# Eight changes at once in the front of a transformer block: chunks of 128 instead of 127 tokens, reordered loads, gate products in column tiles, a longer look-ahead for weight buffers

## Chip, cores, metric

One Trainium2 chip, one program on all 8 of its cores. Times are device microseconds (us) of the slowest core. Cores 0 to 3 are one die, 4 to 7 the other. In some executions, whatever the kernel, one die runs at a lower granted clock and the program takes some per cent longer (the slow state); such runs are set apart, and fast runs are compared with fast runs.

## The reference

A decoder block on `x` of 4 x 2048 x 2048, float32:

```
h = RMSNorm(x)
[B, C, u | q, k, v, o, i, f] = h @ W_in             # i, f: 4 gate columns each
y_m = sigmoid(o) * headnorm(mLSTM(q, k, v, i, f))   # 4 heads, state carried along the sequence
x  += concat(B * conv3(C * u), y_m) @ W_out
x  += W_down(silu(g) * u),  [g, u] = conv3(RMSNorm(x) @ W_up) + b
x  += sigmoid(RMSNorm(x) @ W_pg) * (p @ W_pp)       # the last stage ("PLE")
out = RMSNorm(x)
```

The mLSTM is a linear recurrence with exponential gates: the state that a later token sees is a gated sum of `v_s k_s^T` over all earlier tokens.

## The kernel before

Core `2b + half` has batch `b` and one half of its sequence (1032 tokens with an overlap of 8). Nothing is exchanged between cores. A core of the second half must know the state at the end of the first half, so every core first works through the 1016 tokens before its own (the prefix; zeros for the first half). The front, 0 to some 180 us, runs in this order:

1. Prefix: 8 chunks of 127 tokens. Per chunk: 16 one-column products that sum the squares (for the RMSNorm), 16 products of 8 columns for the gates, 2 x 16 products of 256 columns for the keys (weights k0 and k1), 16 transposes of x.
2. The core's own tokens, half 0: squares on ScalarE, summed on TensorE; logarithm and exponential for 1/rms; sixteen VectorE operations that scale x to h; gate products; then the key unit k0.
3. The big product G = x^T k (16 x 8 products of 512 columns), at position 21 to 28 of the weights' schedule.
4. Rest of the key units, gate mathematics, C = G^T W_v for head 0 (weights v0), then the unit o0. From there to the end the work is mostly bound by TensorE.

The prefix, cut:

```python
LP, NPCH = 127, PT // LP                     # PT = 1016: 8 chunks
def prefix_k(pump):
    slab_load(1, [k1.loads[1]])              # slab c: x of chunk c; slab 1 waits for two loads of k1
    slab_load(2, [k1.loads[3]])              # slab 2 for all of k1
    for c in range(3, 7): slab_load(c)
    ...
    for c in range(NPCH):
        for k in range(16): mm(PS[0:P_, 6, c:c+1], sqd[:, k, :], ones_bf[:, 0:1], ...)           # 127 weights, 1 column
        if c == 0:
            ... own_load(0, f) ... own_load(1, f)       # own x, 2 x 16 transfers
            own.squares(0); Norm.blocks(own, H1, 0, ... own.gates ...)   # queued for ScalarE, VectorE, TensorE
        for k in range(16): mm(PS[0:P_, 6, 16+8*c:24+8*c], hTp[:, c, k, 0:P_], wif[:, k, :], ...) # 8 columns
        for half in range(2):
            for k in range(8*half, 8*half+8):
                for j, p in enumerate((k0, k1)): mm(PS[0:P_, b+j, 0:256], hTp[:, c, k, 0:P_], w, ...)
            ... 8 transposes into bank 7, copied out by VectorE or ScalarE ...
```

The gates (8 weights, the rest of the array idle), the C product and the start of the gate mathematics:

```python
s_mm(PS[0:8, b, 0:QE], wif[:, kk, :], H1.ap(...), kk == 0, kk == 15, ...) for kk in range(16)   # 258 columns each
...
p, b = ip["v%d" % h], 4 + h % 2                                    # c_step(h)
for k in range(16): mm(PS[:, b, 0:256], gT[h][:, k, :], w, ...)    # w: two blocks side by side
...
b = 4                                                              # gate_math
i = later(ops, 1, pre + bank_rd.pop(b, []))     # small transposes of the gates, issued when their turn comes
```

All weights go through slots of 2 KB per partition. A slot is chosen when the program is built, and GpSimd starts the loads strictly in order, each when its slot comes free:

```python
lu = last use of this block + 1;  st = its first use         # positions in the schedule, 7 per unit
s = min((s for s in slots if lu <= s.hi), key=lambda s: (max(s.free, st - 21), s.hi))
```

Slots that are free 21 positions ahead of the first use tie, and the tie goes to the one that stops existing soonest.

## Time and profile before

| | before |
|---|---|
| median of the first 5 runs | 1664.68 us (1663.71 to 1667.09) |
| cores in the profiled run | 1648.6 to 1665.5 us |
| mean granted clock of TensorE | 0.972 to 0.980 |
| TensorE busy on the slowest core | 1538.0 us |

The view of the cores, before:

```profile
core 4: 1665.5 us, clock 0.972
...
die 0 (median of its cores): 1654.9 us, clock 0.977
die 1 (median of its cores): 1661.5 us, clock 0.975
```

The slowest core has the lowest mean clock; both dies are within 0.4%. To see a front of 180 us in a span of 1665 one needs marks that can be found on every core. I use five, all from the timeline: the start of the two logarithms of half 0's squares on ScalarE; the eviction of the first gate product; the start of the last eviction of G; ScalarE's first eviction of o0; and the last load of an activation table on ScalarE, just ahead of the last stage. All stretches are read from one profiled execution of each kernel: where two executions of the same kernel are there, their means over the cores differ by up to 0.6 us in a stretch, by 1.3 us in the long one and by 2.4 us in the span (the change and run 5).

### The profile page before, as it was taken

Reading aid. Unit: us, or ns where it says so; the run is one execution under the profiler, and the core shown is the slowest. Engines: PE = TensorE matmul, PEld = TensorE weight load, DVE = VectorE, ACT = ScalarE, POOL = GpSimd, SP = SyncE. Lnnn points to the kernel's source line nnn. Section 1 sums busy time; section 2 is a strip of 40 time slices with the busy share of each in tenths; the row PEclk is TensorE's granted clock in tenths of the full one; section 3 lists DMA queues with packets and bytes.
Section 4 is the critical chain, followed back from the end, with each engine's and each line's share of the span. In section 5 each row is a group of like instructions: output and inputs, shape, how many; then the busy total and the mean of one; then the engine's idle time right before and its main releaser. Section 6 shows DMA issues by size and latency. Waiting matters only on the chain.

```text
span 1665.5 us, 36629 instructions; the slowest of 8 cores (1648.6 to 1665.5 us)
## 1 busy us (share of the span) xinstructions
PE 1538.0 (92%) x13538; PEld 1289.4 (77%) x13538; DVE 1191.7 (72%) x1817; ACT 607.1 (36%) x1072; POOL 248.4 (15%) x472
## 2 busy tenths in 40 slices
PE   3998999999998996999999999999999997997983
PEld 3965788888877885888888888888888886765762
DVE  1482332477767787887788878888778887977875
ACT  2642225577421223443034510544203543223452
POOL 1001021011121011112211122111221112120100
PEclk9999899999999998999999999999999999998997
DMA  9804564545967353565775558566566565464613
GB/s 202 264 1 78 76 88 65 85 55 71 214 84 110 50 77 47 76 82 65 89 101 79 75 73 107 79 86 86 77 89 97 79 85 77 66 86 66 91 70 133
DMA packets 80782, 149.15 MB, mean 90 GB/s; under 512 B 9184, under 2 KB 25696, under 8 KB 80608
## 3 DMA queue, kind: packets, MB, share of 16 engines
q0 software_dynamic: 67648, 112.82, 50.6%
q1 hardware_dynamic: 12960, 34.00, 6.6%
q8 instruction: 111, 1.82, 0.5%
q14 instruction: 63, 0.52, 0.1%
HBM read 251.18 MB, written 8.39 MB: 156 GB/s over the span
## 4 chain that ended last, share of the span: by engine, by line
PE 81%; DMA 7%; DVE 5%; issue 4%; ACT 2%; POOL 0%; DVEq 0%; ACTq 0%; POOLq 0%
PE PS L330 80%; DVE M L311 3%; DVE M L315 3%; DMA M<-w_in_p 2%; ACT M L306 2%; DMA M<-w_down_p 1%; DMA M<-pT 1%; PE PS L326 1%; DMA M<-w_pg_p 1%; DMA M<-w_out_p 1%; DMA M<-cst_i 1%; POOL M L566 0%; DMA M<-w_up_p 0%; ACT L306 0%; DVEq L211 0%
## 5 line engine op out<-in xcount | busy, mean ns | idle before, releaser
L330 PE MATMUL PS<-M 128*128 128x258 bf16 (+6 forms) x13230 | 1525.1, 275 | 107.6 <-DVE M L311 39.3
L330 PEld LDWEIGHTS PS<-M 128*128 128x128 bf16 (+4 forms) x13230 | 1270.1, 101 | 354.9 <-issue 167.7
L311 DVE TENSOR_TENSOR M<-M 128x512 bf16<-128x512 bf16 (+17 forms) x723 | 499.6, 710 | 70.5 <-PE PS L330 26.5
L306 ACT ACTIVATE M<-PS 128x516 f32<-128x516 f32 (+9 forms) x492 | 241.7, 500 | 578.0 <-PE PS L330 564.4
L315 DVE SCALAR_TENSOR_TENSOR M<-M 128x1024 f32<-128x1024 f32 (+9 forms) x379 | 362.9, 1002 | 54.5 <-ACT M L306 53.3
L306 ACT ACTIVATE M<-M 128x1024 f32<-128x1024 f32 (+10 forms) x402 | 316.6, 815 | 216.3 <-DVE M L311 168.9
L311 DVE TENSOR_TENSOR M<-M,PS 128x512 f32<-128x512 f32 (+6 forms) x444 | 256.6, 580 | 115.3 <-PE PS L330 111.6
L311 DVE TENSOR_TENSOR M<-PS,M 128x516 f32<-128x516 f32 (+10 forms) x194 | 104.5, 543 | 150.1 <-PE PS L330 137.5
L566 POOL DMA_DIRECT2D M<-w_up_p x176 | 93.1, 529 | 477.2 <-PE PS L330 239.0
L566 POOL DMA_DIRECT2D M<-w_in_p x96 | 50.9, 534 | 415.8 <-PE PS L330 328.2
L306 ACT ACTIVATE PS<-PS 128x516 f32<-128x516 f32 (+1 forms) x57 | 32.1, 562 | 219.2 <-PE PS L330 219.2
L566 POOL DMA_DIRECT2D M<-w_down_p x128 | 67.7, 530 | 246.9 <-PE PS L330 185.5
L306 ACT ACTIVATE M<-PS,M 116x256 bf16<-116x256 bf16 (+4 forms) x76 | 34.7, 475 | 15.5 <-PE PS L330 10.8
L1107 DVE COPY M<-PS 127x1024 bf16<-127x1024 bf16 x8 | 5.5, 690 | 44.7 <-PE PS L326 44.7
L566 POOL DMA_DIRECT2D M<-w_pg_p x32 | 17.0, 535 | 105.8 <-PE PS L330 98.6
L566 POOL DMA_DIRECT2D M<-w_out_p x32 | 16.9, 533 | 71.0 <-PE PS L330 49.5
L326 PE MATMUL PS<-M 128*127 128x128 bf16 (+4 forms) x308 | 23.4, 224 | 0.0
L326 PEld LDWEIGHTS PS<-M 128*127 128x127 bf16 (+4 forms) x308 | 22.1, 131 | 0.4
L306 ACT ACT_TABLE_LOAD x9 | 11.5, 1283 | 12.0 <-DMA M<-xsl 9.0
L315 DVE SCALAR_TENSOR_TENSOR M<-M,PS 128x256 f32<-128x256 f32 x28 | 12.6, 474 | 0.8 <-PE PS L330 0.7
L1174 DVE COPY M<-PS 128x256 f32<-128x256 f32 x4 | 1.7, 424 | 14.5 <-PE PS L330 14.5
L994 DVE CAST M<-M 128x128 bf16<-128x128 f32 x1 | 0.2, 227 | 10.8 <-DMA M<-cst_i 10.8
(19 smaller groups left out, 15.4 us busy)
## 6 DMA issues: line engine op xcount, KB each, us to landing
M<-w_up_p POOLq DMA_DIRECT2D x176, 256.0 KB, 5.7
M<-w_in_p POOLq DMA_DIRECT2D x96, 256.0 KB, 6.9
M<-w_down_p POOLq DMA_DIRECT2D x64, 192.0 KB, 4.5
M<-w_down_p POOLq DMA_DIRECT2D x64, 160.0 KB, 4.0
M<-xr SPq DMA_DIRECT2D x32, 258.0 KB, 7.5
M<-xr SPq DMA_DIRECT2D x16, 516.0 KB, 9.5
M<-w_out_p POOLq DMA_DIRECT2D x32, 256.0 KB, 7.0
M<-w_pg_p POOLq DMA_DIRECT2D x32, 256.0 KB, 7.6
```

What stands on the lines that cost most here:

```text
L306: return ("act", lambda e: e.activation(out=out, in_=in_, func=func, **kw), reads, writes, c)
L311: return ("dve", lambda e: e.tensor_tensor(out=out, in0=in0, in1=in1, op=op), reads, writes, c)
L315: return ("dve", lambda e: e.scalar_tensor_tensor(out=out, in0=in0, scalar=scalar, in1=in1, op0=op0, op1=op1), reads, writes, c)
L326: return ("pe", lambda e: e.transpose(out, in_, ident), reads, writes, 0.065)
L330: return ("pe", lambda e: e.matmul(out, lhsT=lhsT, rhs=rhs, start=start, stop=stop, skip_group_check=skip), reads, writes, c)
L566: p.loads.append(P.op("pool", lambda e, d=d, sr=sr: e.dma_start(out=d, in_=sr), [], [p.R[nm]], dma=True, cost=p.KT * 0.25, after=g))
L994: P.op("dve", lambda e: e.tensor_copy(out=ones_bf, in_=onesF), [Rcst], [Rcbf])
L1107: it = later(("dve", lambda e, o=tr_out, i=tr_in: e.tensor_copy(out=o, in_=i), [RPS[7]], tr_R, 1.2), 0)
L1174: read_bank(later(("dve", lambda e: e.tensor_copy(out=E32[:, h, :], in_=PS[:, b, 0:256]), [RPS[b]], [RE32[h]], 0.42), 0), b)
```

## The change

Its intent is to shorten the front. All of its parts, cut to the core (index arithmetic and host-side padding left out):

```diff
-LP = 127
-NPCH = PT // LP
+LP = 128
+NPCH = (PT + LP - 1) // LP                          # x padded with 8 zero tokens in front
...
-            s = min(..., key=lambda s: (max(s.free, st - 21), s.hi))
+            s = min(..., key=lambda s: (max(s.free, st - 28), s.hi))
...
+    act(rsp, rsp, AF.Square, ...)                   # an activation table loaded early
+    ip["k1"].gate = ...                             # k1 is loaded after slab 1
...
-s_mm(PS[0:8, b, 0:QE], wif[:, kk, :], ..., kk == 0, kk == 15)
+s_mm(PS[32*(kk%4):32*(kk%4)+32, b, 0:QE], wif[:, kk, :], ..., kk < 4, kk > 11)   # wif padded to 32 columns
-s_mm(PS[0:LS[c], b, 8*c:8*c+8], gfm[0:8, ...], tct[0:8, TC_ID:TC_ID+8], ...)
+s_mm(PS[0:LS[c], b, 8*c:8*c+8], gfm[:, ...], tct[:, TC_ID:TC_ID+8], ...)         # adds the four partial sums
...
-        slab_load(1, [k1.loads[1]])
-        slab_load(2, [k1.loads[3]])
-        for c in range(3, 7): slab_load(c)
+        slab_load(1, [k0.loads[2]])
+        slab_load(2)
+        pump()
+        slab_load(3, [k1.loads[2]])
+        for c in range(4, 7): slab_load(c)
...
+        for c in range(3): first(c); keys(c, [0])   # squares, gates and k0 of chunks 0 to 2
+        for c in range(3): keys(c, [1])             # their k1 and transposes
+        for c in range(3, NPCH): first(c); keys(c, [0, 1])
...
-            p, b = ip["v%d" % h], 4 + h % 2
+            p, b = ip["v%d" % h], 5 - h % 2         # and C as 2 x 16 products of 128 columns
...
         i = later(ops, 1, pre + bank_rd.pop(b, []))
+        need(i)                                     # gate transposes at once
...
-        slots.append(Slot(RB + 43008 + 2048 * i, (ple0 + 3) * 7, INF))
+        slots.append(Slot(RB + 43008 + 2048 * i, (ple0 + 4) * 7, INF))
```

## The prediction

> **What bounds the kernel now.** I read the page first, then the windows of 20 us, then the timeline and the chain of waits where the windows show TensorE idle. The page says TensorE is busy 1538.0 of 1665.5 us, and its strip shows where it is not:
>
> ```profile
> PE   3998999999998996999999999999999997997983
> DMA  9804564545967353565775558566566565464613
> ```
>
> One slice is 41.6 us. The first slice is the worst (3), and the DMA engines are full there (9, then 8). From about 180 us to 500 us and from 660 to 1380 us TensorE is nearly always busy; the change touches little there. So its worth is read from the front, 0 to 180 us. The timeline of the first 45 us:
>
> ```profile
> 12.46 3.54 PE L330 MATMUL PS<-M 128*127 128x1 bf16 x32 [12.46 <-ACT M L306]
> ...
> 20.63 0.45 PE L330 MATMUL PS<-M 128*127 128x256 bf16 x1 [4.63 <-DMA M<-w_in_p]
> 23.52 6.50 SPq L982 DMA_DIRECT2D M<-xsl  x7
> ...
> 26.11 3.43 PE L330 MATMUL PS<-M 128*127 128x256 bf16 x15 [5.04 <-DMA M<-w_in_p]
> ```
>
> TensorE waits for the key weights of both pairs (k0 at 20.6, k1 at 26.1 us); the second slab of x is asked for only at 23.5 us. Then come seven more chunks of the prefix. One of them:
>
> ```profile
> 51.62 3.61 PEld L330 LDWEIGHTS PS<-M 128*127 128x127 bf16 x48
> 51.68 3.80 PE L330 MATMUL PS<-M 128*127 128x1 bf16 x48
> ...
> 55.73 1.73 PEld L330 LDWEIGHTS PS<-M 128*127 128x127 bf16 x16
> 55.79 1.91 PE L330 MATMUL PS<-M 128*127 128x256 bf16 x16
> ...
> 58.01 3.80 PE L330 MATMUL PS<-M 128*127 128x1 bf16 x48
> ```
>
> A chunk lasts 58.01 - 51.68 = 6.33 us without a gap: TensorE bound. The window of 75 to 80 us is the last with DMA (share 0.78, then 0.01), so the own x of half 0 (half of the last 32 transfers, 258 KB each at about 290 GB/s, 0.9 us each) landed near 65 us, but its squares ended only at 78 us, as they stand in order behind the chunks. The next lines are the end of that stage and the stall after the big G product:
>
> ```profile
> 78.48 0.86 ACT L306 ACTIVATE M<-PS 128x258 f32<-128x258 f32 x2 [0.65 <-PE PS L330]
> ...
> 91.80 2.64 PE L330 MATMUL PS<-M 128*8 128x258 bf16 x11 [0.40 <-DVE M L315]
> ...
> 94.66 15.52 PE L330 MATMUL PS<-M 128*128 128x258 bf16 x159 [0.22 <-ACT M L306]
> ```
>
> ```profile
> 147.62 1.69 POOL L566 DMA_DIRECT2D M<-w_in_p  x3 [13.22 <-PE PS L330]
> ...
> 166.12 0.69 DVE L311 TENSOR_TENSOR M<-M 128x1024 bf16<-128x1024 bf16 x1 [5.91 <-DMA M<-w_in_p]
> 166.73 0.42 DVE L311 TENSOR_TENSOR M<-M,PS 128x258 bf16<-128x258 f32 x1
> ...
> 167.29 5.41 PE L330 MATMUL PS<-M 128*128 128x258 bf16 x26 [5.89 <-DVE M L311]
> ...
> 174.29 1.00 PE L330 MATMUL PS<-M 116*116 116x36 f32 x4 [1.59 <-ACT M L306]
> 176.44 3.79 PE L330 MATMUL PS<-M 128*128 128x256 bf16 x17 [1.15 <-ACT M L306]
> ```
>
> Read it so: the loads of v0 and o0 go to space that G reads, so they start when G ends (147.0). VectorE, in order, stands at o0's first weight sum until its data land (166.1), and the eviction behind it (166.73) holds TensorE. Then gate mathematics and the C product run one after another with waits, on a clock of 0.59 (window 160 to 180, PE busy 11.37 of 20). The unit o0 begins near 179.6 us (176.44 and 16 products at about 0.2 on the cold clock).
>
> **What the Trainium skill says.** "TensorE: Matmul & The Clock Gate", section "Weight-path perf modes", has fast weight load on when the number of weights is 128 and the type is not FP32. The trace agrees: of the 6.33 us of a chunk, 32 products of 256 columns take 3.49 (109 ns each, as in 1.73 us for 16), so the 48 short instructions with 127-column weights take 2.84 us, 59 ns each; the 32 one-column products with 128-column weights in this group take 0.9 us, 28 ns each:
>
> ```profile
> L330 PE MATMUL PS<-M 127*128 127x1 bf16 x32 | 0.9, 164 | 0.0
> ```
>
> The same page, "The HAM clock gate", says an idle TensorE falls to half clock; the 0.59 agrees. "TensorEngine Tiling (Array Packing)", "Tiling Modes" and "Restrictions", says column tiles run in parallel, that changing the mode drains the array, and that column tiling excludes fast weight load; no column tile is in this trace.
>
> **The change part by part.**
> (1) Chunks of 128 tokens instead of 127. Per chunk 32 short products fall from 59 to 28 ns (1.0 us) and 16 transposes of 128 columns to about 56 (0.05 us): 6.33 becomes 5.3 us, 8.3 us over eight chunks. It lies on the path, as far as data are there.
> (2) Loads reordered: k0, slabs 1 and 2, then k1; keys of chunks 0 to 2 with k0 alone first. The DMA moves the same bytes. Written rates were about 119 GB/s for weights in 10 to 26 us and 290 GB/s for x. I get k0 at 17 us, slab 1 at 20.5, slab 2 at 24, k1 at 31.5 (5 us later than now), slab 7 at 49.5, own x of half 0 at 65, as now. TensorE then does three second halves of keys (16 products and 16 transposes, 2.7 us each) from 31.5 to 39.6, where now it has done 1.4 chunks. Five chunks of 5.3 and 32 products of squares at 0.109 (3.5 us) give 69.6. ScalarE needs in a late chunk 1.9 + 1.5 us for squares and copies and some 2.1 for own squares, 5.5 us, so I add 1.4: the prefix ends at 71, against 86.9.
> (3) What follows is not TensorE bound: squares end at 71, logarithm and exponential 1.7 us, sixteen VectorE blocks from 80.30 to 91.66 now (11.4 us), last gate products and their eviction 3.0 us now, perhaps 1.9 with tiles. k0 of half 0 starts at 71 + 1.7 + 11.4 + 1.9 = 86 instead of 94.66: 8.7 us. So about half of the 16 us won on the prefix is given back to this chain.
> (4) Gates in four column tiles: 48 gate products remain after that start, 48 x 0.109 = 5.2 us; four at a time with some drain about 1.7. From there to the end of G TensorE has no gap now (52.4 us), so 3.5 us are kept. G ends at 86 + 52.4 - 3.5 = 135, 12 us earlier.
> (5) Slots of weights preferred when free 28 positions ahead instead of 21. v0 is first used at position 49, and the slots that G frees open at 28. With 21 these tie with ring slots free from the start and win by their end; with 28 ring slots win. So v0's four loads move from 147 to about 65 to 75 us, and o0 is alone after G. Six loads took 18 us there, so o0's first two should take 9 to 10 us after G, and the eviction is never held: the last k1 unit ends 14.9 us after G (it started at 155.87 and has 56 products of 0.109, 6.1 us: 162.0 less 147.0).
> (6) Gate transposes forced early, C in another bank, C as 32 products of 128 columns (32 x 56 ns = 1.8 us, as 16 x 109 now). Warm transposes 2.0, C 1.8, rest 1.2: o0 starts about 20 us after G, now 32.6. Gain 12.6 us.
> (7) The early activation table load (1.28 us) lies before the wait for k0: nothing. The later slot start near the end: within 3 us either way.
> Sum: 12 + 12.6 = 24.6 us. After that all is TensorE bound and keeps it: 1664.7 - 24.6 = 1640.
>
> **The rivals.** (a) The prefix gain is lost entirely: squares of own x, in order on ScalarE behind copies, or the later k1, hold the start of k0 near 92. For it: DMA share 0.9 and over until 75 us and ScalarE busy 4.2 to 4.9 of 5 us in 60 to 80. Against: own x lies there 13 us unused now. Time: 1647 to 1650. (b) The chain starts when own x lands (65), without the lag: k0 at 80, and the late PLE stage gains too (TensorE waits 6.0 us there for pT behind gate weights whose slots change). Time: 1628 to 1633. (c) v0's loads gain nothing, for a new wait comes at o0: its four loads still start after G, two x rows of 516 KB share the DMA, and VectorE blocks again. Then some 5 us remain of 12.6: 1647. (d) Column tiles serialise or drain: 48 products at 109 ns stay, minus 3.5: 1644.
>
> **Range and chances.** The cores differ: core 1 came through the v0 stall 4 to 6 us sooner than core 4, so the slowest core gains more there than the others, and the range is not wider below than above. 1640 us, range 1627 to 1653. The 2% line is 1631.4; only rival (b) gets there. Faster by over 2%: 0.22; within: 0.77; slower: 0.01.
>
> **What would show it.** Short products at 28 to 30 ns and chunks near 5.3 us after 45 us; k1 landing near 31 us; the prefix over near 71; k0 of half 0 near 86; the gates at a quarter of their time; w_in_p loads of v0 between 60 and 90 us; the G product over near 135; no eviction behind a DMA wait after it, the clock near 1.0 there; o0 20 us after G; the same spans afterwards. I am wrong if the chunks stay above 6 us, if TensorE idles over 18 us between prefix and k0, if v0 still loads after G, or if stages after 200 us change by over 4 us.

## The result, and the profile after

| | before | after |
|---|---|---|
| median of all runs on the first chip | 1665.0 us (15 runs) | 1637.1 us (9 runs) |
| ratio of fast runs, 95% interval | | 0.9831 (0.9822 to 0.9841) |
| slowest core, profiled run | 1665.5 us (core 4) | 1636.2 us (core 0) |
| TensorE busy there | 1538.0 us | 1516.1 us |

A ratio is the mean time of one kernel's fast runs over the mean of the other's fast runs of the same rounds, so it is not quite the ratio of the medians. The kernel is 1.7% faster, 28 us: predicted 1640, measured 1637. Whether it came from where it was expected is another question.

The same two rows of the page's strip, after (one slice is 40.9 us):

```profile
PE   3889999999999996999999999999999997998984
...
DMA  8925463345767153555665557555566556554523
```

The first slice is as empty as before (3). The second and third fell from 9 to 8: less work there, and still waits. The fourth, where the stall after G lay, rose from 8 to 9. The last slice rose from 3 to 4.

The front of core 0, now the slowest, after (timeline; start, duration, engine, line, operation, and in brackets the idle time before it and what ended it):

```profile
18.97 20.89 SPq L981 DMA_DIRECT2D M<-xsl  x7
...
20.27 3.57 PE L330 MATMUL PS<-M 128*128 128x256 bf16 x16 [5.08 <-DMA M<-w_in_p]
...
25.24 2.13 POOL L566 DMA_DIRECT2D M<-w_in_p  x4 [20.38 <-DMA M<-xsl]
...
38.17 1.03 PE L330 MATMUL PS<-M 128*128 128x256 bf16 x8 [4.03 <-DMA M<-w_in_p]
```

k0 is there at 20.3 us, as before (20.6 on core 4), and not at the 17 of the prediction. Slab 1 is asked for only at 19.0, k1 only at 25.2, when slab 1 has landed, and k1 is there at 38.2, against 26.1 before and 31.5 in the prediction. The load queue is not full meanwhile. Two windows of 5 us of core 0 (window, length, busy time of TensorE, weight load, VectorE, ScalarE, GpSimd, granted clock, DMA share, GB/s written):

```profile
15.00:20.00 5.00, 0.19 (x8) 0.10 (x4) 0.00 (x0) 0.00 (x0) 0.00 (x0) 1.00 0.52 89
35.00:40.00 5.00, 1.83 (x18) 1.65 (x19) 0.04 (x1) 0.00 (x0) 0.00 (x0) 0.94 0.46 129
```

DMA share 0.52 and 0.46: each load waits until another has landed, and the 16 engines run half empty between. TensorE is busy 1.83 of 5 us in the second.

The end of the prefix on the same core, after:

```profile
65.39 6.08 ACT L306 ACTIVATE M<-M 128x516 bf16<-128x516 f32 x8
71.38 1.49 ACT L306 ACTIVATE M<-PS 128x512 bf16<-128x512 f32 x2
72.76 3.99 ACT L306 ACTIVATE M<-M 128x516 bf16<-128x516 f32 x5
76.65 0.85 ACT L306 ACTIVATE M<-PS 128x258 f32<-128x258 f32 x2
...
77.92 2.71 PE L330 MATMUL PS<-M 128*128 128x1 bf16 x48
...
83.98 0.61 PE L326 MATMUL PS<-M 128*128 128x128 bf16 x8 [1.15 <-DVE M L1113]
...
89.98 1.35 PE L330 MATMUL PS<-M 128*32 128x258 bf16 x11 [0.29 <-DVE M L315]
```

Three things are to be seen. The group of 48 products (32 short ones and 16 of 256 columns) takes 2.71 us (3.80 before). ScalarE goes from own squares (128x516) to copies and back to squares without an idle moment, until the logarithms at 76.65; TensorE is full there too (4.92 to 5.00 us of each 5 from 65 to 80), so which of the two holds the logarithms is not shown. They start at 78.5 before (core 4; 77.6 on core 0) and at 76.7 here; on core 4 at 70.95. And the last transposes of the prefix end at 84.6 us, 8 us after the logarithms started. Before, on core 4, it was much the same (87.0 and 78.5):

```profile
86.40 0.63 PE L326 MATMUL PS<-M 128*127 128x128 bf16 x8
```

So the prefix was over at 85.2 to 87.0 us before (eight cores, mean 86.1) and is over at 78.1 to 86.3 (mean 82.1) now; the prediction had 71. Then the gates: eleven products of 258 columns in 1.35 us, where eleven took 2.64 us before.

The stall after G, after, core 0:

```profile
73.43 2.12 POOL L566 DMA_DIRECT2D M<-w_in_p  x4 [46.07 <-DMA M<-xr]
...
141.40 3.47 POOL L566 DMA_DIRECT2D M<-w_in_p  x6 [13.01 <-PE PS L330]
...
155.43 0.69 DVE L311 TENSOR_TENSOR M<-M 128x1024 bf16<-128x1024 bf16 x1 [1.91 <-DMA M<-w_in_p]
...
156.94 23.23 PE L330 MATMUL PS<-M 128*128 128x258 bf16 x214 [1.78 <-DVE M L1215]
...
167.25 0.58 ACT L306 ACTIVATE PS<-PS 128x516 f32<-128x516 f32 x1 [1.48 <-PE PS L330]
```

Four loads (v0) are issued at 73.4, once the own x has landed; before they stood in line at 147.6. VectorE still waits for weights on this core, but 1.9 us instead of 5.9. From 156.94 TensorE works 23 us without a break: the end of the key units, gate mathematics, C and the start of o0. The window of 160 to 180 us answers to the one with 11.37 us of TensorE and a clock of 0.59 before:

```profile
160.00:180.00 20.00, 20.00 (x191) 18.11 (x191) 6.99 (x15) 5.54 (x12) 3.26 (x7) 0.86 0.46 70
```

Core 0 is the exception here, and it is the core that ends last: o0's first eviction (167.25) comes 24.9 us after the last of G (142.39), against 19.7 to 20.3 us on the other seven. TensorE waited 1.78 us before 156.94, and from 160 to 165 us it is busy but at half the clock:

```profile
160.00:165.00 5.00, 5.00 (x42) 4.82 (x42) 0.39 (x2) 0.77 (x4) 0.00 (x0) 0.50 0.80 139
```

On core 4, where TensorE did not wait, the clock in the same part (150 to 155 us) was 1.00 and 66 products ran in 5 us.

The five marks over all cores, each the mean of the eight, as lengths between them:

| stretch (us) | before | after | difference |
|---|---|---|---|
| start to the logarithms of half 0 | 77.6 | 74.2 | -3.4 |
| to the first gate eviction | 15.6 | 14.3 | -1.3 |
| to the last eviction of G | 55.2 | 52.0 | -3.2 |
| to the first eviction of o0 | 32.4 | 20.4 | -12.0 |
| to the last table load | 1316.5 | 1315.5 | -1.0 |
| to the end | 159.8 | 154.7 | -5.1 |
| sum | 1657.1 | 1631.0 | -26.1 |

Nearly half of the gain is the stall after G. The stretch to the logarithms gave less than half of what was expected (78.5 to 71), and 5 us came from the end of the kernel, where I had expected nothing. So three questions are open: why the start gave so little; whether the parts are worth what the sum says; and what moved the end.

In the table of the cores one more thing is hidden: after the change the cores fall into two groups. Cores 0, 2, 5 and 6 have k1 at 37.9 to 38.3 us and the logarithms at 76.7 to 78.3; cores 1, 3, 4 and 7 have k1 at 34.4 to 35.6 and the logarithms at 70.1 to 72.3. Before, the logarithms lay within 76.6 to 78.5 on all eight. The core that ends last is of the late group.

### The profile page after: what moved, and what is told of

The parts are those of the page before. It is cut to its first block, busy times and chain, and to the rows that moved or that the text cites. A ratio compares the mean times of both kernels' runs of the same rounds, so it can differ in the third digit from the quotient of the medians.

```text
span 1636.2 us, 36766 instructions; the slowest of 8 cores (1626.2 to 1636.2 us)
## 1 busy us (share of the span) xinstructions
PE 1516.1 (93%) x13580; PEld 1267.4 (77%) x13602; DVE 1192.5 (73%) x1819; ACT 608.5 (37%) x1076; POOL 248.4 (15%) x472
## 4 chain that ended last, share of the span: by engine, by line
PE 80%; DMA 7%; DVE 5%; issue 4%; ACT 2%; POOL 1%; SPq 0%; DVEq 0%; ACTq 0%; POOLq 0%
PE PS L330 80%; DVE M L311 3%; DVE M L315 2%; DMA M<-xr 2%; DMA M<-w_in_p 2%; ACT M L306 2%; DMA M<-w_out_p 1%; DMA M<-w_down_p 1%; DMA M<-w_up_p 1%; PE PS L326 1%; POOL M L566 0%; DMA M<-xsl 0%; ACT L306 0%; SPq L981 0%; DVEq L211 0%
## 5 line engine op out<-in xcount | busy, mean ns | idle before, releaser
L330 PE MATMUL PS<-M 128*128 128x258 bf16 (+7 forms) x13272 | 1502.9, 273 | 97.3 <-DVE M L311 35.1
L330 PEld LDWEIGHTS PS<-M 128*128 128x128 bf16 (+3 forms) x13294 | 1249.1, 99 | 342.9 <-issue 154.7
L311 DVE TENSOR_TENSOR M<-M 128x1024 bf16<-128x1024 f32 (+14 forms) x724 | 500.8, 710 | 91.5 <-PE PS L330 33.9
L306 ACT ACTIVATE M<-PS 128x516 f32<-128x516 f32 (+11 forms) x495 | 242.4, 498 | 562.2 <-PE PS L330 549.8
L311 DVE TENSOR_TENSOR M<-PS,M 128x516 f32<-128x516 f32 (+10 forms) x194 | 104.6, 544 | 138.4 <-PE PS L330 126.7
L326 PE MATMUL PS<-M 128*128 128x128 bf16 (+4 forms) x308 | 22.8, 221 | 4.9 <-DVE M L1113 4.1
L326 PEld LDWEIGHTS PS<-M 128*128 128x128 bf16 (+4 forms) x308 | 20.1, 111 | 7.1 <-issue 6.4
L1113 DVE COPY M<-PS 128x1024 bf16<-128x1024 bf16 x8 | 5.5, 689 | 22.4 <-PE PS L326 22.4
L315 DVE SCALAR_TENSOR_TENSOR M<-M,PS 128x256 f32<-128x256 f32 x28 | 12.6, 474 | 0.7 <-PE PS L330 0.7
L995 DVE CAST M<-M 128x128 bf16<-128x128 f32 x1 | 0.2, 228 | 10.7 <-DMA M<-cst_i 10.7
L306 ACT ACTIVATION_READ_ACCUMULATOR M<-PS 116x1 f32 (+1 forms) x36 | 7.2, 201 | 0.0
```

The costliest lines, as they stand in the source:

```text
L306: return ("act", lambda e: e.activation(out=out, in_=in_, func=func, **kw), reads, writes, c)
L311: return ("dve", lambda e: e.tensor_tensor(out=out, in0=in0, in1=in1, op=op), reads, writes, c)
L315: return ("dve", lambda e: e.scalar_tensor_tensor(out=out, in0=in0, scalar=scalar, in1=in1, op0=op0, op1=op1), reads, writes, c)
L326: return ("pe", lambda e: e.transpose(out, in_, ident), reads, writes, 0.065)
L330: return ("pe", lambda e: e.matmul(out, lhsT=lhsT, rhs=rhs, start=start, stop=stop, skip_group_check=skip), reads, writes, c)
L995: P.op("dve", lambda e: e.tensor_copy(out=ones_bf, in_=onesF), [Rcst], [Rcbf])
```

## The experiments

Twelve runs, in four calls, each call on a chip of its own beside the kernel before; all gave correct outputs. Theory: each part removes the wait or the work that the prediction names for it, and the gains add up. Rivals: the reordered loads are what helps (or hurts) the prefix; gains of the front are lost again; the end gains by itself. In most runs one part is undone in the changed kernel. The changed kernel's own ratio is 0.9831 on the first chip and 0.9838 in the second call; 0.001 is 1.7 us.

**1. Look-ahead back to 21** (first call)

```diff
-key=lambda s: (max(s.free, st - 28), s.hi)
+key=lambda s: (max(s.free, st - 21), s.hi)
```

> The changed kernel with the slot preference back at 21 positions, all else kept. The recorded prediction (front only, tail within 3 us): v0's four loads go back behind the G product, so the stall after G returns in part, some 5 to 8 us, and the late stage moves by under 3 us: 1642 to 1646. Rival, formed after seeing the changed trace (w_pp and pT are issued 6 to 10 us before the last activation table load there instead of 2.5): the preference also feeds the late stage; then 5 to 8 us at the front and 6 to 10 us at the end are lost: 1648 to 1655, with w_pg loads standing ahead of w_pp again.

Measured: 1645.7 us median, ratio 0.9901 (0.9887 to 0.9914), so 10.5 to 11.6 us of the gain are lost (by the two ratios of the change). Core 4, this run:

```profile
143.41 2.93 POOL L566 DMA_DIRECT2D M<-w_in_p  x5 [0.30 <-issue]
...
158.12 0.69 DVE L311 TENSOR_TENSOR M<-M 128x1024 bf16<-128x1024 bf16 x1 [4.11 <-DMA M<-w_in_p]
...
171.22 0.58 ACT L306 ACTIVATE PS<-PS 128x516 f32<-128x516 f32 x1 [1.43 <-PE PS L330]
```

v0's loads are back behind G, VectorE waits 4.1 us for weights with an eviction behind it, and o0 comes 28.8 us after the last G eviction (142.43) instead of 19.7 on this core in the change. The mean of that stretch is 24.9 us (19.9 to 29.0; 20.4 in the change), and the end takes 158.1 us instead of 154.7. So the look-ahead is worth some 4.5 us in the mean and up to 9 us on single cores at the front, and 3 us at the end. In the two profiles the mean span is 6.5 us and the slowest core 8.0 us longer than in the change; the ratios say 10.5 to 11.6, as on this chip the kernel before is some 3 us faster than on the first. Expected were 5 to 8 us at the front, where it is 4.5 in the mean; the end moved by 3.4 us, a little more than the prediction's "under 3" and well under the rival's 6 to 10.

**2. Chunks of 127 again** (first call)

```diff
-LP = 128
+LP = 127
```

> The changed kernel with chunks of 127 tokens. Recorded prediction: short products go from 28 back to 59 ns, 1.0 us per chunk; 8.3 us of TensorE time in all, of which about half reaches the start of k0: plus 4 to 6 us, 1641 to 1643. Rival: the prefix is bound by the arrival of k1 and of own x and not by TensorE, then plus 0 to 2 us, 1637 to 1639, though the products are as slow as before.

Measured: 1641.5 us, 0.9881 (0.9864 to 0.9899): 7 to 8 us lost, more than the 4 to 6 expected. The short products, core 0:

```profile
56.80 3.80 PE L330 MATMUL PS<-M 128*127 128x1 bf16 x48
```

3.80 us for 48, as before the change. The logarithms start at 76.8 us in the mean instead of 74.2: seven of the eight cores are now as late as the late half was in the change (75.3 to 78.3). That is 2.6 us. The stretch to o0 is 0.8 us and the end 2.0 us longer than in the change, which the edit doesn't touch; 1.2 us of the latter is TensorE waiting for pT (see run 9), on five cores instead of one. The mean span is 4.9 us longer than in the change's profile and 7.2 us longer than in run 5's, the same kernel on another chip; so one execution of each can't divide the 7 to 8 us any further.

**3. The old loads, with chunks of 128** (first call): `prefix_k` as before, and no wait of k1 for slab 1.

```diff
-        slab_load(1, [k0.loads[2]])
-        slab_load(2)
-        slab_load(3, [k1.loads[2]])
-        for c in range(4, 7): slab_load(c)
+        slab_load(1, [k1.loads[1]])
+        slab_load(2, [k1.loads[3]])
+        for c in range(3, 7): slab_load(c)
...  # keys of k0 and k1 together in every chunk
-    ip["k1"].gate = lambda: [dm["slab", 1]] if ("slab", 1) in dm else None
```

> The changed kernel with the loads and the order of keys of the kernel before (k0 and k1 first, then the slabs; both halves of the keys of a chunk together), chunks of 128 kept. Recorded prediction: the new order hides three chunks' first halves and own x lands at 65 us either way, so undoing it costs about 5 us: 1642. Rival: in the new order the DMA engines idle (share 0.46 to 0.68 in 15 to 20 and 30 to 40 us) so that own x lands 67 to 73 us instead of 65; then undoing it costs nothing or gains: 1634 to 1638, with k1 landing near 26 us and own x near 65.

Measured: fast runs 1637.3 us median, 0.9851 (0.9834 to 0.9868), against 0.9831 and 0.9838 for the change: the intervals overlap, the reordering is worth some 2 to 3 us by the means and perhaps nothing; I had expected 5, and the rival (nothing or a gain) came nearer. The logarithms start at 72.4 us in the mean, sooner than in the change (74.2), and on all cores within 70.9 to 73.9: the two groups are gone. The prefix is over at 78.8 to 81.8 us (mean 80.4; 82.1 in the change). Where its data are there a chunk takes what the prediction gave it (core 0, two chunks; the second line is 5.19 us after the first, predicted 5.3, 6.33 before):

```profile
43.01 2.71 PE L330 MATMUL PS<-M 128*128 128x1 bf16 x48
...
48.20 2.71 PE L330 MATMUL PS<-M 128*128 128x1 bf16 x48
```

**4. k1 free of slab 1** (first call): the order of the change, but k1 does not wait for slab 1, nor slab 3 for k1.

```diff
-    ip["k1"].gate = lambda: [dm["slab", 1]] if ("slab", 1) in dm else None
-        slab_load(3, [k1.loads[2]])
+        slab_load(3)
```

> The changed kernel with the two gates taken away that let the DMA idle: k1 is loaded straight behind k0 and slab 3 does not wait for k1. If the idle DMA is what kept k0 of half 0 at 85 to 92 us instead of the recorded 86, own x lands near 65 us in every core, k1 near 30, the logarithm of the squares near 69 to 71, and the time falls 3 to 7 us: 1630 to 1634. Rival: squares stand in the order of ScalarE and TensorE behind the chunks, so an earlier own x changes nothing: 1636 to 1638.

Measured: fast runs 1641.8 us median, 0.9876 (0.9862 to 0.9891): slower than the change by 6 to 8 us. My expectation was wrong. Core 3, window and timeline:

```profile
25.00:30.00 5.00, 0.00 (x0) 0.00 (x0) 0.00 (x0) 0.00 (x0) 0.00 (x0) 0.79 1.01 285
```

```profile
32.05 1.91 ACT L306 ACTIVATE M<-M 128x2048 bf16<-128x2048 f32 x1 [7.43 <-DMA M<-xsl]
34.10 4.32 PE L330 MATMUL PS<-M 128*128 128x1 bf16 x48 [9.96 <-ACT M L306]
...
65.31 2.13 POOL L566 DMA_DIRECT2D M<-w_in_p  x4 [52.51 <-DMA M<-xr]
...
78.09 0.39 ACT L306 ACTIVATE M<-PS 128x258 f32<-128x258 f32 x1
```

The DMA is full (1.01), but slab 1 lands only at 32 us (23 on this core in the change), and all engines of the core are idle from 25 to 30. Two waits were taken away, so slab 1 now shares the DMA engines with k1 and with the slabs behind it; what of the delay comes from which is not separated. The own x has landed at 65.3, earlier than in the change (67.2 on this core), and the logarithms start no sooner, at 78.1 (70.1 there). So it is not the arrival of the own x that sets them: its squares stand behind the chunks, and the chunks behind slab 1.

**5. The change itself** (second call)

The changed kernel, unedited, for its ratio on this chip.

> The changed kernel itself, unaltered, as the yardstick of this chip for the other three runs of this call. Both theories: a ratio to the kernel before of 0.983, as when it was first measured (0.9822 to 0.9841).

Measured: six of eight runs slow; the two fast ones 1634.8 and 1635.1 us, 0.9838 (0.9819 to 0.9856). The two groups are here again, but on other cores: k1 at 37.1 to 37.5 us on cores 0, 2, 4 and 7, at 33.8 to 35.0 on 1, 3, 5 and 6.

**6. Gates in one group of columns** (second call)

```diff
-PS[32*(kk%4):32*(kk%4)+32, b, 0:QE], wif[:, kk, :],   ..., kk < 4, kk > 11
+PS[0:8, b, 0:QE],                    wif[:, kk, 0:8], ..., kk == 0, kk == 15
```

> The changed kernel with the gate products back in one group of 8 columns, 16 in a row, instead of four column tiles. Recorded prediction: 48 of them stand on TensorE's path at 109 ns instead of a quarter of it, so plus 3.5 us against the changed kernel, and the 16 of the first gate add under 1 us more. Rival (mode changes drain the array, and TensorE waits for the VectorE blocks there anyway): plus 0 to 1 us.

Measured: two fast runs, 1638.6 us, 0.9859 (0.9841 to 0.9878): 3.5 us lost by the means, with intervals that overlap that of run 5. The gate products between 60 and 180 us, by groups (busy us, mean ns; idle before), first before on core 4, then after on core 0, then this run on its slowest core:

```profile
L330 PE MATMUL PS<-M 128*8 128x258 bf16 x64 | 9.7, 293 | 2.9 <-DVE M L315 2.9
```

```profile
L330 PE MATMUL PS<-M 128*32 128x258 bf16 x64 | 5.2, 334 | 3.1 <-DVE M L315 3.1
```

```profile
L330 PE MATMUL PS<-M 128*8 128x258 bf16 x64 | 10.7, 313 | 3.2 <-DVE M L315 3.2
```

One product is no shorter in a tile (334 against 293 to 313 ns); four run at once. Over all 64 the engine is busy half as long and not a quarter, as the first products come one by one behind VectorE (the 3 us of idle time before them). The 32 of half 1, which wait for nothing, show the tiles alone (100 to 140 us, before on core 4, then after on core 0):

```profile
L330 PE MATMUL PS<-M 128*8 128x258 bf16 x32 | 3.7, 273 | 0.0
L330 PE MATMUL PS<-M 128*32 128x258 bf16 x32 | 1.1, 274 | 0.0
```

By the starts in the trace one product follows another after 110 ns before; after, four start within 10 ns and the next four 110 ns later. That is the quarter. The stretches agree, on all eight cores: from the logarithms to the last G eviction it is 70.7 us here (69.9 to 71.5) and 70.8 before, 66.3 in the change (65.7 to 66.9).

**7. Gate mathematics as before** (second call)

```diff
         i = later(ops, 1, pre + bank_rd.pop(b, []))
-        need(i)
...
-            p, b = ip["v%d" % h], 5 - h % 2
+            p, b = ip["v%d" % h], 4 + h % 2
```

> The changed kernel with the gate transposes not forced early and the C product back in the bank of the gate mathematics. Recorded prediction, step 6: the waits of 1.59 and 1.15 us and the cold clock of that stage return in part, plus 3 to 5 us. Rival: once v0 is loaded early there is no stall, the clock stays up, and the order of these small products costs under 1.5 us.

Measured: 1639.3 us median, 0.9862 (0.9848 to 0.9876): 4 us lost. From the last G eviction to o0 it is 25.1 to 25.4 us on all eight cores (19.7 to 20.6 in the change on this chip). The waits of before are back, core 0:

```profile
160.80 0.85 PE L330 MATMUL PS<-M 116*116 116x36 f32 x4 [1.59 <-ACT M L306]
```

**8. Old loads, and another bank for k0 of half 0** (second call): edit 3, and

```diff
-bk = [nx, 2 - 2*((un+1)%2) + s, 4 + s, 1 - s]
+bk = [nx, 2 - 2*((un+1)%2) + s, 6 if p.name == "k0" and s == 0 else 4 + s, 1 - s]
```

> The changed kernel with the loads and key order of the kernel before, and with k0 of half 0 accumulating in bank 6 instead of bank 4. Theory: the start of k0 is held by the whole chain of 16 VectorE blocks only because bank 4 holds the first gate, so that k0 (64 products, 7 us) waits for the gate and its eviction; in bank 6 k0 follows the blocks one by one and ends with them. Then o0 starts 5 to 7 us earlier in each core, and the time is 5 to 7 us under the changed kernel: a ratio of 0.979 to 0.980. Rival: VectorE's sums for k1, which come after the blocks, are the bound from there on, and the gain is under 2 us.

Measured: fast runs 1636.0 us median, 0.9845 (0.9831 to 0.9859). k0 needs no longer wait for the eviction of the gates, but TensorE then runs into the next wait, for VectorE's weight sums (core 1):

```profile
84.10 13.90 PE L330 MATMUL PS<-M 128*128 128x258 bf16 x156 [1.91 <-DVE M L311]
101.48 45.87 PE L330 MATMUL PS<-M 128*128 128x258 bf16 x301 [2.80 <-DVE M L311]
```

The last G eviction comes at 138.4 us in the mean (139.0 in run 3, on another chip). The wait moved; of the 5 to 7 us that I had expected nothing shows in the time (0.9851 in run 3).

**9. The last stage's small loads four half units earlier** (third call)

```diff
# in the last group of the down projection
+        if g == 3: us[8].pre = lambda: pp_load()      # w_pp and pT
# in the first unit of the last stage
-            if n == 0: pp_load()
```

> The changed kernel with w_pp and pT asked for four half units earlier, when the first half of the last product's activations (whose space they take) has been read. Theory: the 151 to 159 us that cores need after the last activation table load differ by the wait for pT behind gate weights, which the look-ahead of 28 shortened but did not end; without it all cores take 151 to 153 us and the time falls 2 to 5 us against the changed kernel: a ratio of 0.980 to 0.982. Rival (recorded prediction: the late stage is worth under 3 us and the spread has other causes): under 1 us, 0.983 to 0.984, with the spread as before.

On this chip the second die was slow in every run, before (1684.3 us) as in the rest, so there is no ratio of fast runs. The first die was undisturbed: the median of its slowest core is 1630.8 us (7 runs), 1659.7 for the kernel before; for the change it was 1634.2 on the first chip and 1633.0 in the second call, and the kernel before had 1659.3 and 1659.5 in the first two calls. So 2 to 3 us, across chips. The profile says where. Issue of w_pp and pT and the table load ahead of the last stage, before on core 4:

```profile
1495.00 0.70 POOL L1659 DMA_DIRECT2D M<-w_pp  x1 [2.60 <-DMA M<-w_pg_p]
1497.74 0.71 POOL L1660 DMA_DIRECT2D M<-pT  x1 [2.04 <-DMA M<-w_pg_p]
1500.23 1.28 ACT L306 ACT_TABLE_LOAD   x1
...
1517.01 11.01 PE L330 MATMUL PS<-M 128*128 128x512 bf16 x67 [6.01 <-DMA M<-pT]
```

after on core 4:

```profile
1463.52 0.71 POOL L1680 DMA_DIRECT2D M<-w_pp  x1
1464.21 0.73 POOL L1681 DMA_DIRECT2D M<-pT  x1
1474.09 1.28 ACT L306 ACT_TABLE_LOAD   x1
```

and in this run on core 0:

```profile
1445.45 0.71 POOL L1682 DMA_DIRECT2D M<-w_pp  x1 [31.75 <-PE PS L330]
...
1479.17 1.28 ACT L306 ACT_TABLE_LOAD   x1
```

pT is asked for 2.5 us ahead of the table load before, 9.9 us after, 33 us here (2.5 to 7.5, 7.1 to 9.9 and 33.0 over all cores). These loads stand in order on GpSimd behind gate weights (w_pg_p) that wait for slots; the longer look-ahead gave those weights slots that come free sooner. In run 1, with the look-ahead of 21, pT leads by 3.6 to 6.4 us. TensorE's wait for pT in the last stage follows: 2.8 to 6.6 us before (mean 4.7), 0.2 to 6.3 in run 1 (mean 3.5), none on seven cores after and 2.7 us on core 5 (mean 0.3). So does the end of the kernel: 159.8 us before, 158.1 in run 1, 154.7 after. Here it takes 150.7 to 151.6 on the first die, though the change had no wait for pT there any more; TensorE's waits for VectorE and ScalarE in the last stage are 1.7 us shorter, for a reason that was not followed up.

**10. Every second square on VectorE** (third call): edit 3, and

```diff
-s_act(self.sq[s][i], stage[s][f], AF.Square, ...)
+s_tt(self.sq[s][i], stage[s][f], stage[s][f], ALU.mult, ...) if s == 0 and f % 2 else s_act(... AF.Square ...)
```

> The changed kernel with the loads and key order of the kernel before, and every second square of half 0's own x made on VectorE instead of ScalarE. Theory: own x lands near 65 us there, but its squares end at 71 to 74 us because ScalarE has copies and squares to do; with half of them on VectorE, idle then, the logarithm comes near 68 and o0 starts 3 to 5 us earlier than with the old loads alone (157 to 163 us): 154 to 159, the time 2 to 4 us under 1636. Rival: the squares stand in TensorE's order behind the chunks and ScalarE is not what holds them: no change, o0 at 157 to 163 us.

The first die's slowest core: 1632.6 us (8 runs), against 1635.2 for run 3 on another chip. The logarithms start at 70.5 to 72.9 us (70.9 to 73.9 in run 3; I had expected 68). A small gain is possible; it can't be told from the difference of chips. Inconclusive.

**11. Together: runs 3, 8, 9 and 10** (third call)

The four edits in one kernel.

> The parts that the experiments favour together: old loads, k0 of half 0 in bank 6, half of the squares on VectorE, w_pp and pT early. Theory: the gains add, 3 to 5 us from the front and 2 to 5 us from the late stage: 1626 to 1631 us, ratio 0.978 to 0.981. Rival: other waits, the VectorE sums for k1 and the spread between cores[...], take the gain back: 1633 to 1636, 0.983.

The first die's slowest core 1628.4 us (8 runs) against 1659.7 before; the second die slow again. So it was run once more on another chip:

**12. The same kernel** (fourth call)

> The combined kernel once more, in the hope of a chip without a slowed die, for the call before had one throughout. From the undisturbed die there (its slowest core 1628.4 us in the median, against 1659.7 for the kernel before and 1633 to 1634 for the changed kernel on other chips) both theories are already narrowed: if the parts add, 1629 to 1632 us and a ratio of 0.980 to 0.982; if what die 0 showed was that chip only, 1634 to 1636 and 0.983 to 0.984.

Measured: 1631.3 us median, before 1663.2 us, ratio 0.9806 (0.9793 to 0.9819): 32 us, 4 to 5 us more than the change. The logarithms start at 71.8 us in the mean, the last G eviction comes at 137.4, o0 at 158.3, and the end takes 151.9. This is the fastest version found; it has the old order of loads in it.

## Why the prediction was right or wrong, by its own steps

The sum was near (24.6 us predicted, 26 in the mean of the cores, 28 for the kernel), two of its terms were wrong, and they cancelled. Of its own signs of being wrong two came true: a stage after 200 us changed by over 4 us (the end), and a chunk took over 6 us on five of the six cores where one can be read.

| stretch (mean of 8 cores, us) | before | after | after, run 5 | look-ahead 21 | chunk 127 | old loads | one gate group | gate mathematics old |
|---|---|---|---|---|---|---|---|---|
| to the logarithms | 77.6 | 74.2 | 73.6 | 73.2 | 76.8 | 72.4 | 72.5 | 73.1 |
| to the last G eviction | 70.8 | 66.3 | 66.0 | 66.1 | 66.0 | 66.6 | 70.7 | 66.3 |
| to o0 | 32.4 | 20.4 | 19.8 | 24.9 | 21.2 | 21.0 | 20.1 | 25.3 |
| the end | 159.8 | 154.7 | 155.0 | 158.1 | 156.7 | 155.6 | 154.5 | 155.5 |

Each undone part but the loads brings back the stretch that it was said to shorten; the other stretches move by up to 1.7 us, the end by up to 2.0.

- **Step 1, chunks of 128: right.** Short products: a group of 48 takes 2.71 us; 16 of them are 256-column products at 0.109 (1.75 us), so the other 32 take 0.96 us, 30 ns each (by the same working 64 before, from 3.80 us; the prediction's 59 and 28 are from starts). A chunk with its data there takes 5.19 us (predicted 5.3; run 3). In the change itself the chunk that follows the three split ones took 5.6 to 7.9 us on the six cores where it can be read; on core 0 TensorE waits 1.58 us behind VectorE in it. "TensorE: Matmul & The Clock Gate", section "Weight-path perf modes" of the Trainium skill, which put this on the number of weights, held. Worth 7 to 8 us to the kernel by run 2, of which the stretch to the logarithms shows 2.6 in the mean.
- **Step 2, the loads: the step that failed at the front.** Predicted k0 at 17, k1 at 31.5, the own x at 65, the prefix over at 71, and with it the squares. Measured k0 at 19.1 to 20.3, k1 at 34.4 to 38.3, the own x at 67 to 73.4 (core 0), the prefix over at 78.1 to 86.3. Core 0 term by term: k1 is 6.7 us late; the three second halves take 12.3 us (38.2 to 50.5) and not 8.1, as TensorE waits for copies of its transposes (1.38 us behind VectorE) at a granted clock of 0.72; the last five chunks take 34.1 us (50.5 to 84.6) and not 31.4. That makes the 13.6 us. I had reckoned with a DMA that never stands still; but in the new order loads wait for other loads to land, and the share falls to 0.46 to 0.52 (0.64 on core 4). k1's four loads need 12.9 us from being asked for to the first product (the prediction gave them 7.5; it also puts the weights' rate in 10 to 26 us at 119 GB/s, where the trace has 143). And the prediction set the end of the squares equal to the end of the prefix. The traces keep them some 8 us apart, before (78.5 and 87.0 on core 4) as after: the logarithms come first. So that they start at 70.1 to 72.3 us on the early cores, and at 72.4 in the mean with the old order (run 3), near the predicted 71, is luck: the prefix is over at 80.4 in run 3. The 71 was some 9 to 11 us too early for the end of the prefix, and was used for an event that comes 8 us before it. Run 4 shows that removing the two waits is no cure, as slab 1 then lands at 32 us.
- **Step 3, the chain behind: the shape held.** From the logarithms to the first gate eviction it is 14.27 to 14.29 us on all cores, early or late. Its start was wrong, by step 2: k0 of half 0 starts at 85.0 to 87.2 us on the early cores (predicted 86) and at 91.6 to 93.2 on the late ones; so G ended 8 us sooner in the mean, not 12. On core 4, of the early group, it was 10.8 us.
- **Step 4, the gates: right.** 4.5 us in the stretches (4.4 by those of run 6), 1.3 to the first gate and 3.2 from there to the end of G (predicted 1.1 and 3.5); 3.5 us by run 6. Products that wait for nothing run at a quarter of the time. The drain of rival (d) does not show.
- **Step 5, the look-ahead: right in mechanism.** v0's loads moved from 147 to 67 to 73 us. "The eviction is never held" is true on six cores; on core 0 the wait fell from 5.9 (core 4) to 1.9 us, and with the halved clock behind it it costs this core 5 us. It is worth 10.5 to 11.6 us to the kernel (run 1), of which the prediction had a part in step 6.
- **Step 6, gate mathematics and C: right.** 20.4 us from G to o0 in the mean (predicted 20; 19.7 on six cores, 24.9 on core 0), 12.0 us less than before (predicted 12.6). Of this run 7 gives 5 us to the two small edits, run 1 4.5 us and more to the look-ahead. That C is split in two halves could not be taken back alone without touching the slots.
- **Step 7, the end: wrong.** Predicted: within 3 us. Measured: -5.1 us in the mean, -13 us on core 4. I had ranked it as a rival (the late stage gains too, since weights there change their slots) and given it little. The look-ahead acts on every weight of the kernel, not on v0 alone, and w_pp and pT stand behind it in the queue. TensorE's wait for pT fell by 4.4 us in the mean (4.7 to 0.3), which is most of the 5.1; run 1 brings 3.1 us of this wait and 3.4 us of the end back. Rival (b) had named this very wait and its cause; the sum left it out. What the later start of four slots (`ple0 + 4`) does was not tried alone.

The rivals: (a) 1647 to 1650, the prefix gain lost, k0 held near 92: true for the front of the four late cores (91.6 to 93.2), not for the time. (b) 1628 to 1633: its first half (the chain starts at 65) did not happen, its second half did. (c) v0's loads still behind G: no; a new wait at o0 only on core 0, and smaller. (d) tiles that serialise: no.

So 1640 was met because two errors cancel: some 4 to 5 us too much at the front, 5 too little at the end; and in the front the 71 itself is partly luck (step 2). The costs of undoing single parts, by ratios, are 11 (look-ahead), 7 to 8 (chunk), 3.5 (gates), 4 (gate mathematics) and 0 to 3 (loads): 26 to 30 us, against the 28 of the whole. They nearly add up, as parts that lie one behind another on the same path would.

Open: what a single part is worth in the kernel before (every part was taken back inside the change, and the early table load and the later slots not at all; chunks of 128 alone in the kernel before were not run, and a look-ahead of 28 alone does not compile there, as the C product reads two weight blocks in one access pattern and the new slots lie too far apart); which of k1's and the slabs' loads hold each other up; and why one core of a pair is late.

## What to carry to other kernels

An order of loads is judged by two readings together, the DMA share and the landing of the transfer that the first waiting engine needs: with loads that wait for each other the share fell to 0.46, with two of the waits taken away it was full and the needed slab came 9 us later. A rule of allocation acts on every buffer of the program, so look at what it does to the far end too, above all to small loads that stand in order behind large ones. And check each term of a sum against its own stretch of the trace: a total that agrees can hide two errors that cancel.

## What the Trainium skill lacked or had wrong

- "TensorE: Matmul & The Clock Gate", "Weight-path perf modes": gives the gain as a factor only ("~2× (measured)"), with no time for a stream of short products. Measured here: 64 ns each with 127 columns, 30 with 128, at one to 8 moving columns; the factor agrees.
- "TensorEngine Tiling (Array Packing)", "Tiling Modes", says that a change of the tiling mode drains TensorE, without a cost. Here 64 gate products in four column tiles, with one-column-group work before and behind, took 5.2 us of busy time against 9.7 to 10.7, and 32 that waited for nothing 1.1 us against 3.7; no run shows a drain worth naming.
- "DMA: Bandwidth & Descriptors", "Issuing engines are not separate DMA queues", says that transfers of different issuing engines interleave on the same 16 engines. Run 4 agrees: slab 1 (issued by SyncE) landed at 32 us with k1 (issued by GpSimd) and the later slabs beside it, at 23 in the change. The page doesn't warn that an order of loads can be spoiled so: here it cost 6 to 8 us against the change.
- No page has why, under the new order of loads, one core of each pair 0/1, 2/3, 4/5, 6/7 gets k1 some 3 to 4 us later than the other (37 to 38 against 34 to 35.6 us) and the logarithms 4 to 8 us later. Which of the two it is differs from execution to execution, on one chip too (the late ones are 0, 2, 5, 6 on the first chip; 0, 2, 4, 7, then 0, 3, 4, 7, then 0, 2, 4, 6 in runs 5 to 7 on another), so it is not fixed to a core. The old order shows no such groups (25.4 to 27.7 us).
